# Twelve column tiles of the input projection by Strassen's seven products, in three waves

## The chip, the cores and the metric

The kernel runs on one core of a Trainium2 chip. The metric is the device time of one execution in microseconds (us). A profile is one execution recorded by the hardware profiler; its span runs from the first to the last recorded instruction and is a little shorter than the device time of that execution. Engines: PE is TensorE's matmuls, PEld its weight loads, DVE is VectorE, ACT is ScalarE, POOL is GpSimd, SP is SyncE, from whose queue this kernel starts its transfers.

## The reference

A decoder trunk of two layers over 1024 tokens of width 1024, all float32. Each layer does, cut to what matters:

```
xn   = rms_norm(h, norm_mix)
proj = xn @ w_in                       # 1024 x 1024 by 1024 x 3120
gq, gk, gv, glr, ggate | cc, cb, ch, cgate | cq, ckv, kr, mgate = split(proj)
o_gla  = gated linear attention(gq, gk, gv, glr), normed, times silu(ggate)
o_conv = cb * causal_conv3(cc * ch) * silu(cgate)
o_mla  = softmax attention(rms_norm(cq) @ w_uq, rms_norm(ckv) @ w_ukv, kr) * silu(mgate)
h = h + concat(o_gla, o_conv, o_mla) @ w_out
h = h + cross_attention(rms_norm(h), mem)
```

The last line of the network is one more rms_norm. The change concerns the columns cc, cb, ch, cgate, cq and ckv of `proj`, 256 columns each.

## The kernel before, in words

Activations are kept transposed: a tile is 128 features by 512 tokens, so a layer's activations are 8 feature tiles in 2 halves of the tokens. Each float32 operand is split into a high part in a shorter format and the rest, and one product is three matmuls, high by high, high by low and low by high (`mm3`, L298 to L303). The input projection's columns are laid out as 25 tiles of 128. `win` (L393) computes one of them: it loads the 1024 x 128 weights (512 KB, `wraw`), casts the high part on ScalarE and subtracts it for the low part in two halves on GpSimd or VectorE (`wsplit`; tiles with number 3 modulo 4 go to VectorE), and for each half of the tokens accumulates 8 x 3 matmuls of 128x512 in one PSUM bank, which VectorE evicts with the norm's factor R (L402). Raw weights have 2 buffers (tag "wr"), split parts 6 (tag "w").

Per layer: first the tiles of the linear attention's q, k and v; then its front; then the state loop, `gla_body` for two head pairs in four rounds. In each round the program takes steps from a list called `fill` between the bodies' steps: the attention gates, the linear attention's gates (`gate`, which writes the finished gate to DRAM) and the first convolution group (`conv`, four tiles). After the loop come `latent` for ckv (tiles 20 and 21) and cq (18 and 19), the rotary keys, the first keys and the second convolution group, and then the softmax attention, the output projection and the cross-attention.

Tiles come from pools with tags: "s" has 64 tiles of 128x512, "p" 9, "pt" 4. A new tile waits until one of its tag is free. The eight PSUM banks are tagged "mm" (1), "S" (4), "t" (2) and "v" (1). The order of the instructions on each engine is set before the run by a planner that simulates the program with modelled costs; at run time each engine, and the SP queue, goes through its list in that order and waits where an operand or a buffer is not ready. `hd` in DRAM holds the residual stream, which `absorb` writes for each feature tile.

## Time and profile before

| | us |
|---|---|
| median of 3 runs | 1417.07 |
| lowest, highest | 1415.62, 1418.71 |
| the profiled execution's own time | 1415.69 |
| its span | 1413.9 |
| PE busy in it | 1382.9 |

The span is what the profile's views divide; the profiled execution's own time is 1.8 us longer. PE's busy time counts overlapping matmuls once. A row of grouped instructions ends with the group's busy time, the mean length of one in ns, and the idle time of its engine just before them with what ended it.

### The profile page before, as it was taken

What the parts mean: (1) busy time and instruction counts of PE and PEld (TensorE: products, weight loads), DVE (VectorE), ACT (ScalarE), POOL (GpSimd) and SP (SyncE); (2) the same over time, 40 slices, a digit from 0 to 9 for tenths busy, and PEclk for the clock granted to TensorE, in tenths of its full rate; (3) what the DMA queues carried; (4) which work ended last, traced back from release to release, by engine and by line L of the source; (5) the groups of instructions that cost most, each with busy time, mean ns of one, the idle gap of its engine ahead of it and who ended that gap; (6) DMA issues with size and microseconds to landing.
All of it is one profiled execution on the core that took longest, in us unless ns stands there. A gap on an engine that the chain in (4) does not pass through costs nothing.

```text
span 1413.9 us, 19744 instructions
## 1 busy us (share of the span) xinstructions
PE 1382.9 (98%) x7132; PEld 1128.0 (80%) x7132; DVE 771.0 (55%) x1431; ACT 690.0 (49%) x1462; POOL 571.7 (40%) x584
## 2 busy tenths in 40 slices
PE   7998999999999999999999999999999999999998
PEld 6787888888776688888878788888887767888886
DVE  7846445364788554545653632534657883553533
ACT  5446544253777442555431653424557773344543
POOL 6325335215556452353342532441356663414320
PEclk9999999999999999999999999999999999999999
DMA  8131222122122254321522121211232123534403
GB/s 310 53 129 53 77 76 74 47 63 91 45 61 65 92 172 134 121 89 46 185 100 82 49 78 53 89 58 45 83 86 60 33 81 112 194 105 142 156 1 120
DMA packets 61827, 131.13 MB, mean 93 GB/s; under 512 B 7553, under 2 KB 14497, under 8 KB 61729
## 3 DMA queue, kind: packets, MB, share of 16 engines
q1 hardware_dynamic: 61728, 129.87, 28.5%
q8 instruction: 56, 0.92, 0.3%
q14 instruction: 43, 0.34, 0.1%
HBM read 95.76 MB, written 33.55 MB: 91 GB/s over the span
## 4 chain that ended last, share of the span: by engine, by line
PE 83%; DVE 9%; ACT 3%; issue 2%; DMA 2%; POOL 1%; SPq 0%; DVEq 0%; POOLq 0%; ACTq 0%
PE op_ps L301 4%; PE op_ps L302 4%; PE op_ps L303 4%; PE av L848 4%; PE pt L834 3%; PE xqps L301 2%; PE xqps L302 2%; PE xqps L303 2%; PE s L301 2%; PE gg_ps L301 2%; PE gg_ps L303 2%; PE gg_ps L302 2%; PE s L303 1%; PE s L302 1%; DVE gla_a L479 1%
## 5 line engine op out<-in xcount | busy, mean ns | idle before, releaser
L149 POOL TENSOR_TENSOR win_l<-win_r,win_h 128x512 fp32r<-128x512 f32 x76 | 104.1, 1391 | 196.4 <-ACT win_h L127 191.6
L805 POOL TENSOR_SCALAR p<-p,sm 128x128 f32<-128x128 f32 (+3 forms) x144 | 87.8, 619 | 63.8 <-DVE sm L803 41.5
L127 ACT CAST win_h<-win_r 128x1024 fp32r<-128x1024 f32 x50 | 52.4, 1049 | 123.5 <-PE gg_ps L302 36.6
L303 PE MATMUL op_ps<-mix_h,wout_l 128*128 128x512 f32 x256 | 99.9, 390 | 0.0
L302 PE MATMUL op_ps<-mix_l,wout_h 128*128 128x512 f32 x256 | 99.8, 390 | 0.0
L301 PE MATMUL op_ps<-mix_h,wout_h 128*128 128x512 f32 x256 | 99.0, 393 | 0.0
L799 ACT ACTIVATE p<-s,nm 128x128 f32<-128x128 f32 (+3 forms) x144 | 83.2, 581 | 27.1 <-DVE nm L795 13.8
L791 DVE TENSOR_REDUCE nm<-s 128x1 f32<-128x128 f32 (+3 forms) x144 | 78.4, 551 | 3.1 <-PE s L303 1.1
L834 PE MATMUL pt<-ident,p 128*128 128x128 f32 x432 | 70.6, 280 | 1.6 <-POOL p L805 1.5
L834 PEld LDWEIGHTS pt<-ident,p 128*128 128x128 f32 x432 | 49.7, 140 | 27.3 <-issue 13.7
L848 PE MATMUL av<-ph,V 128*64 128x256 f32 x480 | 69.6, 375 | 0.0
L149 POOL TENSOR_TENSOR wout_l<-wout_r,wout_h 128x512 fp32r<-128x512 f32 x32 | 43.3, 1376 | 42.5 <-ACT wout_h L127 34.4
L301 PE MATMUL s<-k_h,q_h 128*128 128x128 f32 (+3 forms) x144 | 55.2, 386 | 1.3 <-ACT p L799 0.6
L301 PEld LDWEIGHTS op_ps<-mix_h,wout_h 128*128 128x128 f32 x256 | 47.7, 188 | 10.5 <-issue 0.8
L302 PEld LDWEIGHTS op_ps<-mix_l,wout_h 128*128 128x128 f32 x256 | 48.1, 188 | 9.9
L303 PEld LDWEIGHTS op_ps<-mix_h,wout_l 128*128 128x128 f32 x256 | 48.1, 188 | 9.8
L842 ACT COPY ph<-pt 128x512 f32<-128x512 f32 (+1 forms) x72 | 39.6, 549 | 23.7 <-PE pt L834 20.6
L301 PE MATMUL xqps<-op_x_h,wq_h 128*128 128x512 f32 x128 | 51.1, 399 | 0.0
L1005 POOL TENSOR_SCALAR xp<-xp,xsm 128x256 f32<-128x256 f32 x64 | 29.8, 482 | 51.4 <-DVE xsm L1003 51.3
L303 PE MATMUL xqps<-op_x_h,wq_l 128*128 128x512 f32 x128 | 50.4, 393 | 0.0
L302 PE MATMUL xqps<-op_x_l,wq_h 128*128 128x512 f32 x128 | 50.2, 392 | 0.0
L302 PE MATMUL s<-k_l,q_h 128*128 128x128 f32 (+3 forms) x144 | 49.9, 347 | 0.0
(502 smaller groups left out, 4292.5 us busy)
## 6 DMA issues: line engine op xcount, KB each, us to landing
win_r<-in_w_in SPq DMA_DIRECT2D x50, 512.0 KB, 3.6
wout_r<-in_w_out SPq DMA_DIRECT2D x16, 512.0 KB, 4.0
x<-in_x SPq DMA_DIRECT2D x16, 256.0 KB, 6.3
hd<-h SPq DMA_DIRECT2D x16, 256.0 KB, 4.0
op0r<-hd SPq DMA_DIRECT2D x16, 256.0 KB, 4.0
hd<-op0r SPq DMA_DIRECT2D x16, 256.0 KB, 2.9
wq_r<-in_w_mem SPq DMA_DIRECT2D x8, 512.0 KB, 3.8
wk_r<-in_w_mem SPq DMA_DIRECT2D x8, 512.0 KB, 3.6
```

The costliest lines, as they stand in the source:

```text
L127: ins = self.nc.scalar.copy(hi, raw)
L149: eng.tensor_tensor(lo, src, hi.bitcast(F32), op=ALU.subtract)
L301: nc.tensor.matmul(ps, a[0], b[0], start=first, stop=False, **k)
L302: nc.tensor.matmul(ps, a[0], b[1], start=False, stop=False, **k)
L303: nc.tensor.matmul(ps, a[1], b[0], start=False, stop=last, **k)
L791: nc.vector.tensor_reduce(nm[:, b : b + 1], ps[:, :w], axis=AX.X, op=ALU.max, negate=True)
L799: nc.scalar.activation(x[:, :w], ps[:, :w], AF.Exp, bias=nm[:, 0:1], accum_out=sm[:, b : b + 1])
L805: nc.gpsimd.tensor_scalar(pr[b][:, :w], pr[b][:, :w], sm[:, 0:1], 1.0, op0=ALU.mult, op1=ALU.mult)
L834: nc.tensor.transpose(ps[:, o : o + P], prob[qi][kt // 4][:, (kt % 4) * P : (kt % 4 + 1) * P], self.ident,)
L842: nc.scalar.copy(pt[:, :w], ps[:, :w])
L848: nc.tensor.matmul(av[own if j == 0 else other, q0:256], self.V[kt][:, 64 * h : 64 * h + 64], pt[:, j * 256 : j * 256 + 256 - q0], start=( ...
L1005: nc.gpsimd.tensor_scalar(pr[:, j], pr[:, j], sm[:, j : j + 1], 1.0, op0=ALU.mult, op1=ALU.mult)
```

## The change

Twelve tiles per layer leave `win`: the latents' four (18 to 21) and the two convolution groups' eight (10 to 17), as six pairs. For a pair, the output is a 2 x 2 block (two column tiles, two token halves) and the sum over features is cut in two halves of four tiles. Instead of eight block products, each 4 x 3 matmuls, there are seven, by Strassen's scheme in Winograd's form: four sums of activation blocks (`a_side`) and four differences of weight blocks (`w_first`, `w_second`) go into them, and partial products are added to each other as they leave PSUM.

The seven products are done in three waves over all six pairs. `wave1` does three of them with the plain activations and writes two partial products per pair to DRAM (`pd`), the second weights' differences too (`wtd`). `wave2` does two with the sums S2 and S3, reads the partial products back and writes two new ones (`ud`). `wave3` does two with S1 and S4 and reads those. Results go to `Sink` tiles, the convolution's gates through DRAM. `a_side` reads the residual stream from `hd`, scales it by gain and by R, and writes the four sums to DRAM (`sd`); `s_parts` reads and splits them. `conv` and `latent` no longer compute their tiles but take the sinks. The linear attention's gates move ahead of the convolution in `fill`; `a_side`, `wave1` and two of `s_parts` are put into the state loop's rounds. Buffers: "s" from 64 to 59, "pt" from 4 to 5, raw weights from 2 to 4.

```diff
-BUFS = {"s": 64, "p": 9, "pt": 4, "tq": 1}
+BUFS = {"s": 59, "p": 9, "pt": 5, "tq": 1}
...
+PAIRS = ((20, 21), (18, 19), (10, 11), (13, 12), (14, 15), (17, 16))
...
-        raw = self.wp.tile(shape, F32, tag="wr", bufs=2, name=name + "_r")
+        raw = self.wp.tile(shape, F32, tag="wr", bufs=4, name=name + "_r")
...
+    def a_side(self, l):
+        nc = self.nc
+        for k in range(4):
+            t = {}
+            for m, c in ((k, 1), (k + 4, 1), (k, 0), (k + 4, 0)):
+                x = self.g(f"sa{l}_{m}_{c}")
+                nc.sync.dma_start(x, self.hd[m][c])
+                nc.scalar.activation(x, x, AF.Copy, scale=self.gain(l, "mix", m))
+                self.mul(nc.gpsimd, x, x, self.R[c])
+                t[(m // 4, c)] = x
+            a11, a12, a21, a22 = t[(0, 0)], t[(1, 0)], t[(0, 1)], t[(1, 1)]
+            nc.vector.tensor_tensor(a22, a21, a22, op=ALU.add)
+            nc.gpsimd.tensor_tensor(a21, a11, a21, op=ALU.subtract)
+            nc.vector.tensor_tensor(a11, a22, a11, op=ALU.subtract)
+            nc.gpsimd.tensor_tensor(a12, a12, a11, op=ALU.subtract)
+            for j, x in enumerate((a22, a11, a21, a12)):
+                nc.sync.dma_start(self.sd[j][k], x)
+            yield
+    def s_parts(self, l, j):
...
+        for k in range(4):
+            raw = self.g(f"sr{l}_{j}_{k}", tag="pt")
+            nc.sync.dma_start(raw, self.sd[j][k])
+            hi, lo = self.g(f"sh{l}_{j}_{k}", F32R), self.g(f"sl{l}_{j}_{k}", F32R)
+            self.split(hi, lo, raw, eng=self.pick("sp", k))
...
+    def w_first(self, l, n):
...
+        r1, r2 = raws
+        hi, lo = self.wsplit(r1, sh, f"win{l}_{i1}")
+        nc.gpsimd.tensor_tensor(r2[:, :4], r2[:, :4], r1[:, :4], op=ALU.subtract)
+        nc.gpsimd.tensor_tensor(r2[:, 4:], r2[:, 4:], r2[:, :4], op=ALU.subtract)
+        t4 = self.g(f"t4_{l}_{n}", tag="tq", shape=[P, 4, P])
+        nc.vector.tensor_tensor(t4, r1[:, 4:], r2[:, 4:], op=ALU.subtract)
+        nc.sync.dma_start(self.wtd[n], r2)
+        w4 = self.wp.tile(sh, F32R, tag="w", bufs=6, name=f"w4_{l}_{n}")
+        nc.scalar.copy(w4[:, :4], t4)
+        self.sub(nc.vector, w4[:, 4:], t4, w4[:, :4])
...
+    def w_second(self, l, n, j):
...
+        if j == 0:
+            nc.sync.dma_start(r, src)
+            (nc.vector if n % 2 else nc.gpsimd).tensor_tensor(r[:, 4:], r[:, 4:], r[:, :4], op=ALU.subtract)
+            nc.sync.dma_start(r[:, :4], self.wtd[n][:, 4:])
+        else:
+            nc.sync.dma_start(r[:, :4], self.wtd[n][:, :4])
+            nc.sync.dma_start(r[:, 4:], src[:, 4:])
...
+        nc.scalar.copy(hi, r)
+        for h, e in ((0, nc.gpsimd), (4, nc.vector)):
+            self.sub(e, lo[:, h : h + 4], r[:, h : h + 4], hi[:, h : h + 4])
...
+    def wave1(self, l):
...
+        w = self.w_first(l, 0)
+        for n in range(len(PAIRS)):
...
+            self.prod(x, wb, a11, True)
+            p1 = self.g(f"p1_{l}_{n}", tag="pt")
+            nc.vector.tensor_tensor(p1, x, self.R[0], op=ALU.mult)
+            nc.sync.dma_start(self.pd[n][0], p1)
+            yield
+            if n + 1 < len(PAIRS):
+                w = self.w_first(l, n + 1)
+            self.prod(y, w4, a22, True)
...
+            nc.sync.dma_start(self.pd[n][1], p4)
+            yield
+            self.prod(x, lambda k: wb(4 + k), a12, False)
+            s = self.sink[PAIRS[n][0]]
+            nc.vector.tensor_tensor(s.tile(0), x, self.R[0], op=ALU.mult)
+            s.done(0)
+            yield
...
+    def wave2(self, l):
...
+        def head(n):
+            w[n] = self.w_second(l, n, 0)
+            x[n] = self.psum(("S", "mm", "S", "t")[n % 4], f"vx{l}_{n}")
+            p1[n] = self.spilled(l, f"q1_{l}_{n}", self.pd[n][0])
+            self.prod(x[n], w[n][0], s2, True)
+            u = self.g(f"u2_{l}_{n}", tag="pt")
+            nc.vector.tensor_tensor(u, x[n], p1[n], op=ALU.add)
+            nc.sync.dma_start(self.ud[n][0], u)
+        head(0)
+        yield
+        for n in range(N):
+            if n + 1 < N:
+                head(n + 1)
+                yield
+            p4 = self.spilled(l, f"q4_{l}_{n}", self.pd[n][1])
+            self.prod(x[n], w[n][1], s3, False)
+            u = self.g(f"u3_{l}_{n}", tag="pt")
+            nc.vector.tensor_tensor(u, x[n], p1[n], op=ALU.add)
+            nc.sync.dma_start(self.ud[n][1], u)
+            k = self.sink[PAIRS[n][0]]
+            nc.gpsimd.tensor_tensor(k.tile(1), u, p4, op=ALU.add)
+            k.done(1)
+            yield
+    def wave3(self, l):
...
+        def head(n):
+            w[n] = self.w_second(l, n, 1)
...
+            u3 = self.spilled(l, f"v3_{l}_{n}", self.ud[n][1])
+            self.prod(y[n], w[n][0], s1, True)
...
+            nc.vector.tensor_tensor(k.tile(1), y[n], u3, op=ALU.add)
...
             gates = [self.gate(l, 22 + i, self.mgd[i], f"mg{l}_{i}") for i in range(3)]
+            gates += [self.gate(l, 7 + i, self.ggd[i], f"gg{l}_{i}") for i in range(3)]
...
+            sides = self.a_side(l)
+            first = self.wave1(l)
+            fill = chain(*gates[1:])
+            parts = chain(self.s_parts(l, 1), self.s_parts(l, 2))
             bodies = [self.gla_body(l, 0), self.gla_body(l, 1)]
-            for _ in range(4):
+            for r in range(4):
                 for b in bodies:
                     next(b, None)
+                    next(sides, None)
+                    if r > 1:
+                        next(parts, None)
+                        next(parts, None)
                     for _ in range(2):
-                        next(fill, None)
+                        if next(fill, 0) == 0:
+                            next(first, None)
+                            next(first, None)
             for b in bodies:
                 run(b)
-            run(fill)
+            run(sides)
+            weave((first, 1), (parts, 1))
+            last_parts = chain(self.s_parts(l, 0), self.s_parts(l, 3))
+            weave((self.wave2(l), 1), (last_parts, 1))
...
+            third = self.wave3(l)
+            for _ in range(10):
+                next(third, None)
             self.wkn = self.mla_w(l, 2)
-            for _ in range(2):
-                next(conv)
             run(self.krope(l))
+            run(third)
             run(self.mla_k(l, 0))
```

## Rows read from the trace of the kernel before

**Rows 1.** The page: span, and busy time of each engine with its share.
```profile
span 1413.9 us, 19744 instructions
PE 1382.9 (98%) x7132; PEld 1128.0 (80%) x7132; DVE 771.0 (55%) x1431; ACT 690.0 (49%) x1462; POOL 571.7 (40%) x584
```

**Rows 2.** The page: the chain that ended last, share of the span by engine.
```profile
PE 83%; DVE 9%; ACT 3%; issue 2%; DMA 2%; POOL 1%; SPq 0%; DVEq 0%; POOLq 0%; ACTq 0%
```

**Rows 3.** Windows: state loop, then to first keys; layer 1's loop.
```profile
core 0: us, PE busy (x) PEld busy (x) DVE busy (x) ACT busy (x) POOL busy (x), PEclk, DMA share, GB/s
137.00:251.50 114.50, 114.25 (x606) 98.12 (x605) 47.17 (x86) 50.34 (x104) 45.79 (x38) 1.00 0.22 70
251.50:345.00 93.50, 93.03 (x410) 76.63 (x409) 46.17 (x63) 37.17 (x57) 25.90 (x20) 1.00 0.21 65
823.00:937.50 114.50, 114.25 (x607) 98.07 (x606) 47.10 (x86) 50.46 (x103) 45.78 (x38) 1.00 0.22 70
```

**Rows 4.** Timeline of PE in the latents: start us, length us, instruction.
```profile
252.21 0.39 PE L301 MATMUL ckv_ps<-h_x_h,win_h 128*128 128x512 f32 x1
...
257.65 0.39 PE L301 MATMUL ckv_ps<-h_x_h,win_h 128*128 128x512 f32 x1
```

**Rows 5.** Groups of GpSimd, 137 to 251.5 us: busy us, mean ns, idle before.
```profile
L149 POOL TENSOR_TENSOR win_l<-win_r,win_h 128x512 fp32r<-128x512 f32 x14 | 18.4, 1335 | 27.5 <-ACT win_h L127 27.5
L152 POOL TENSOR_TENSOR osq<-osb 128x384 f32<-128x384 f32 x8 | 6.6, 826 | 10.7 <-ACT osb L579 10.7
L152 POOL TENSOR_TENSOR gg<-gg,gg_1s 128x512 f32<-128x512 f32 x2 | 2.6, 1284 | 14.2 <-issue 14.2
```

**Rows 6.** Groups of VectorE in the same stretch.
```profile
L590 DVE TENSOR_TENSOR gv<-osb,oms 128x192 f32<-128x192 f32 x14 | 6.8, 525 | 2.6 <-ACT oms L586 2.6
L402 DVE TENSOR_TENSOR gg<-gg_ps,h_acc 128x512 f32<-128x512 f32 x6 | 4.1, 690 | 15.0 <-PE gg_ps L303 15.0
L412 DVE SCALAR_TENSOR_TENSOR gg_2s<-gg,gg_2s 128x512 f32<-128x512 f32 x2 | 1.9, 950 | 0.9 <-ACT gg_2s L411 0.9
L412 DVE SCALAR_TENSOR_TENSOR gg_1s<-gg,gg_1s 128x512 f32<-128x512 f32 x2 | 1.4, 693 | 0.9 <-ACT gg_1s L411 0.9
L149 DVE TENSOR_TENSOR win_l<-win_r,win_h 128x512 fp32r<-128x512 f32 x2 | 1.3, 684 | 0.0
```

**Rows 7.** Groups of ScalarE over the whole span.
```profile
L127 ACT CAST win_h<-win_r 128x1024 fp32r<-128x1024 f32 x50 | 52.4, 1049 | 123.5 <-PE gg_ps L302 36.6 <-PE gq_ps L302 24.9 <-PE gk_ps L302 16.1
L159 ACT CAST q_h<-tq 128x512 fp32r<-128x512 f32 x24 | 14.9, 620 | 18.1 <-DVE tq L769 17.8
L162 ACT ACTIVATE op_x_h<-op1r,gains 128x512 fp32r<-128x512 f32 x16 | 11.5, 720 | 21.8 <-DVE op1r L926 21.8
```

**Rows 8.** Waits, 130 to 345 us: total us, times, longest.
```profile
POOL win_l L149 <- ACT win_h L127: 58.1, 8, 15.4
```

**Rows 9.** Transfers, 130 to 345 us: total; one issue line.
```profile
DMA packets 7459, 14.70 MB, mean 68 GB/s; under 512 B 893, under 2 KB 2941, under 8 KB 7446
win_r<-in_w_in SPq DMA_DIRECT2D x12, 512.0 KB, 3.6
```

**Rows 10.** The page's transfers: a 256 KB load from the residual stream.
```profile
op0r<-hd SPq DMA_DIRECT2D x16, 256.0 KB, 4.0
```

**Rows 11.** Windows in which the DMA engines are full.
```profile
11.00:16.00 5.00, 4.61 (x15) 3.06 (x14) 4.84 (x6) 4.76 (x8) 4.92 (x4) 1.00 1.04 403
512.00:518.00 6.00, 6.00 (x28) 4.99 (x27) 5.75 (x6) 3.01 (x6) 5.40 (x4) 1.00 1.00 361
690.00:700.00 10.00, 9.64 (x43) 7.66 (x42) 8.84 (x11) 8.03 (x13) 8.00 (x6) 1.00 1.00 347
```

**Rows 12.** Waits of the SP queue, 130 to 345 us.
```profile
SPq L595 <- DVE gv L590: 43.6, 10, 10.2
SPq L120 <- ACT win_h L127: 40.6, 7, 14.9
```

**Rows 13.** GpSimd's weight subtraction: ns min/median/max.
```profile
L149 POOL TENSOR_TENSOR win_l<-win_r,win_h x76: 1264/1299/1927, 11.0 to 1015.0; 128x512 fp32r<-128x512 f32 x76
```

More of the change, by code (lines that the diff above doesn't have):

```diff
@@ new lines, in s_parts, with prod @@
+    def s_parts(self, l, j):
+        nc = self.nc
+        self.Sp[j] = []
+        for k in range(4):
[3 more added lines that the diff above has]
+            self.split(hi, lo, raw, eng=self.pick("sp", k))
+            self.Sp[j].append((hi, lo))
+            yield
+    def prod(self, ps, w, xs, first):
+        for k, x in enumerate(xs):
+            self.mm3(ps, w(k), x, first and k == 0, k == len(xs) - 1, skip_group_check=True)
@@ new lines, in wave1 @@
+    def wave1(self, l):
+        nc = self.nc
+        half = lambda j, c: [(self.x1[4 * j + k][0][c], self.x1[4 * j + k][1][c]) for k in range(4)]
+        a11, a12, a22 = half(0, 0), half(1, 0), half(1, 1)
+        w = self.w_first(l, 0)
+        for n in range(len(PAIRS)):
+            tags = ("S", "S") if n % 2 else ("mm", "S")
+            x = self.psum(tags[0], f"wx{l}_{n}")
+            y = self.psum(tags[1], f"wy{l}_{n}")
+            wb, w4 = w
+            self.prod(x, wb, a11, True)
[6 more added lines that the diff above has]
+            self.prod(y, w4, a22, True)
+            p4 = self.g(f"p4_{l}_{n}", tag="pt")
+            nc.vector.tensor_tensor(p4, y, self.R[1], op=ALU.mult)
+            nc.sync.dma_start(self.pd[n][1], p4)
[5 more added lines that the diff above has]
+            yield
@@ new lines, in wave3 @@
+    def wave3(self, l):
+        nc = self.nc
+        s1, s4 = self.Sp[0], self.Sp[3]
+        N = len(PAIRS)
+        w, y = {}, {}
+        def head(n):
+            w[n] = self.w_second(l, n, 1)
+            y[n] = self.psum(("S", "mm", "S", "t")[n % 4], f"vy{l}_{n}")
+            u3 = self.spilled(l, f"v3_{l}_{n}", self.ud[n][1])
+            self.prod(y[n], w[n][0], s1, True)
+            k = self.sink[PAIRS[n][1]]
+            nc.vector.tensor_tensor(k.tile(1), y[n], u3, op=ALU.add)
+        head(0)
+        yield
+        for n in range(N):
+            if n + 1 < N:
+                head(n + 1)
+                yield
+            u2 = self.spilled(l, f"v2_{l}_{n}", self.ud[n][0])
+            self.prod(y[n], w[n][1], s4, False)
+            k = self.sink[PAIRS[n][1]]
+            nc.vector.tensor_tensor(k.tile(0), y[n], u2, op=ALU.add)
+            k.done(0)
+            k.done(1)
+            yield
+            if n in self.after:
+                yield from self.after[n]
@@ L431, in in_q, with sinks @@
+    def sinks(self, l):
+        self.sink = {}
+        for j in range(2):
+            self.sink[13 + 4 * j] = GateSink(self, self.cgd[j], f"cg{l}_{j}")
+            for i in range(3):
+                self.sink[10 + 4 * j + i] = Sink(self, f"c{i}{l}_{j}")
+        for i in range(18, 22):
+            self.sink[i] = Sink(self, f"lat{l}_{i}")
     def in_q(self, l, p, tags=("mm", "S")):
@@ L672, in latent @@
         nc = self.nc
-        raw = [self.g2(f"{what}{l}_{i}") for i in range(2)]
+        raw = [self.sink[base + i].t for i in range(2)]
         acc = self.g2(f"{what}acc{l}", tag="pt")
         for i in range(2):
-            c = 0
-            for _ in self.win(l, base + i, f"{what}{l}_{i}", lambda c: raw[i][c], PAIR[f"lat{i}"]):
+            for c in range(2):
                 if i == 0:
```

103 lines of the change are left out of this document (66 added, 37 removed).

## The prediction

> **What bounds the kernel now.** I read the page's share of busy time first, then the chain of waits, then the busy times of the two stretches that the change rewrites, then the single instructions and transfers in them. The page has TensorE busy in 98% of the 1413.9 us span [rows 1], and the chain that ended last runs on PE for 83% of it [rows 2]. In the stretches that hold the state loop with its fill (137 to 251.5 us) and the latents, the second convolution group and the first keys (251.5 to 345 us), PE is busy for 114.25 of 114.5 us and 93.03 of 93.5 us at full clock; VectorE, ScalarE and GpSimd are at most half busy and the DMA engines are at 0.21 to 0.22. Layer 1's loop shows the same numbers [rows 3]. So in these stretches time is the number of matmuls times their spacing. A 128x512 matmul is shown as 0.39 us, but its records overlap: 24 of them in a row take from 252.21 to 257.65 us, start to start, which is 5.44/24 = 0.2267 us each [rows 4]. That is the price of one.
>
> **The change part by part.** *TensorE.* A column tile is 2 halves x 8 k x 3 matmuls = 48; twelve tiles are 576 per layer. A pair by seven products is 7 x 4 x 3 = 84, six pairs 504. So 72 matmuls go per layer, 72 x 0.2267 = 16.3 us, and 32.6 us in both. The waves then take 216, 144 and 144 matmuls: 49.0, 32.6 and 32.6 us of PE. The product order gives each accumulation a product (2.7 us) in which its eviction hides.
>
> *GpSimd.* Added per layer: 24 operations of 128x512 for the sums of the activations, 24 in the first weights, 15 in the second and third, 8 in splitting the sums, 6 in the second wave: 77. Gone: the subtractions of nine of the twelve tiles, 18 (three were VectorE's). Net 59 x 1.335 us [rows 5] = 79 us. All the cover there is: GpSimd was busy 45.8 + 25.9 us in the two stretches [rows 3], 208 us long; after it is 151 of 192. What counts is the first part, loop and first wave. It lasts 114.5 - 4 x 48 x 0.2267 + 49.0 = 120 us of PE. GpSimd has there 52 new operations (69.4 us at 1.335), the gates' six subtractions, twelve gate products at about 1.285 and eight squares at 0.826 [rows 5]: 99.5 us, 83%. It sits idle for 58.1 us in eight waits before a weight's subtraction today [rows 8]; that cushion is nearly used up.
>
> *VectorE and ScalarE.* VectorE: 18 more evictions at 0.69, 12 + 15 for weights, 8 + 8 for the sums, less 6: 55 x 0.69 [rows 6] = 38 us per layer on top of 93 in 208. ScalarE: weight casts from 12 x 1.05 to about 22 us, 16 scalings at 0.72 and 16 casts at 0.62 [rows 7]: 31 us more on top of 88. Neither becomes a bound; both hide behind PE as long as their inputs arrive. What is queued behind a late one is the state loop's own eviction and copy.
>
> *DMA.* This is the larger change. The old stretch moves 14.70 MB at a mean of 68 GB/s [rows 9]. Added per layer: 16 loads and 16 stores of 256 KB for the sums, 16 loads to split them, six 512 KB stores and twelve 256 KB stores in the first wave, and in the second wave per pair 512 + 256 + 256 + 256 KB of loads and 2 x 256 KB of stores. The second wave thus moves 6 x 1.835 MB, 8 x 0.262 MB of sums for the third wave and 0.52 MB of gates: 13.6 MB in 32.6 us, which is 418 GB/s. With all 16 engines busy the trace shows 361 and 347 GB/s where loads and stores mix, 403 GB/s where nearly all are loads [rows 11]. 13.6 MB takes 39.2 us at 347 and 33.8 us at 403. So the second wave is short by 1.2 to 6.6 us per layer, less what is fetched ahead: two of the four raw weight buffers (1 MB, 2.9 us at 347) are free when the first wave ends, and the last stores may land in the third wave, which moves some 7.5 MB in 32.6 us (230 GB/s). From below the cost is 0, from above 6.6; I take 3 per layer, nearest to the mixed rows less one prefetch.
>
> *Queue and pool.* All transfers go through SP in order. SP waits today 43.6 us for the state's results and 40.6 us for weight casts without harm [rows 12], because a weight is due only every 10.9 us. Now some 130 more issues stand in the same queue, stores that wait for a result among loads that are due; each wait holds every load behind it. And the pool "s" has 59 tiles: the activations hold 32, the state loop's q, k and v 20, its transposed keys 2 and the rotary rows 2, so 3 are free where the sums want 4 at a time. The first sum therefore waits for the first round of the state loop to give tiles back, and the rest crowds into rounds 3 and 4, where the first weights want GpSimd too. Bounds: 0 if the plan slides under PE, 20 us per layer if GpSimd's 99.5 us become serial with a fifth idle. I take 3. The fewer tiles in the output projection (32 + 32 wanted at its end) cost nothing: the old tiles come free at two per 0.68 us, just as they are wanted. For the third wave and the hand-overs between waves I take 1.5 (nothing at best; at worst one weight load, 3.6 us [rows 9], at each of two hand-overs).
>
> *Sum.* Profiled execution 1415.7 - 32.6 + 2 x (3 + 3 + 1.5) = 1398.1 us. That execution lies 1.4 us under the median of the three runs shown, so I say 1398.
>
> **A rule against it.** VectorE and GpSimd slow each other where both read SBUF: a VectorE gate step of one form took 0.950 us on one tile and 0.693 us on another [rows 6], and one GpSimd subtraction form took from 1264 to 1927 ns [rows 13]. The Trainium skill ("SBUF — State Buffer", section "Who interferes with whom") states that a VectorE instruction with two SBUF inputs and a GpSimd one that reads SBUF lock each other out for the whole instruction. The spread in these rows agrees with it; that every overlap blocks fully they do not show.
>
> **The rivals.** *All hidden:* the planner keeps the transfers and sums under PE as it does now with everything else. For: 98% PE at present, and no idle PE at 137 to 345 us. Against: 418 GB/s is more than any row shows for a mix. Time 1415.7 - 32.6 = 1383.1.
>
> *The shared read port binds the first part:* VectorE's instructions with two SBUF inputs there (12 for weights, 8 sums, 4 splits, 12 gate steps, 2 gate-weight subtractions at about 0.69, 16 at 0.525) are 34.6 us; GpSimd at 1.27, near the least of one form [rows 13], is 95 us. In turn they take 130 us against PE's 120: 10 us per layer instead of my 3. With 4.5 for the rest, 1415.7 - 32.6 + 29 = 1412. For: the rows just named. Against: the means are near the minimum today.
>
> *The second wave runs at the pace of its weights (slower):* its second operand is loaded (3.6 us for 512 KB [rows 9]), differenced (1.3), half of it overwritten by a second load that must wait for that difference (4.0 for 256 KB [rows 10]), cast (1.05) and subtracted (1.3): 11.3 us in series, through one in-order queue, against 5.44 us of PE per pair. Buffers allow about three pairs ahead. If the queue lets it be only one (a store that waits for an eviction stands before the next load), each of 12 pairs waits 11.3 - 5.4 = 5.9 us: 1415.7 - 32.6 + 71 = 1454. It decides from a lead under 8.6 us, where 12 x 2.7 us eats the gain; a lead of 7 us gives 1435. For: DMA engines near full lengthen both loads. Against: the four raw buffers.
>
> *The change does less than it says:* the matmuls are counted out in the code, so I give this no chance.
>
> **How the numbers follow.** My forecast (1390 to 1408) 0.50, all hidden 0.17, the shared port (1408 to 1425) 0.15, the second wave's chain (1420 to 1455) 0.18. What a measurement of this kernel can tell from no change is about 0.2%, 2.8 us. Faster: 0.50 + 0.17 + a third of the port case, about 0.72. Within 0.2%: 0.07 out of the port case. Slower: the chain and the port's tail, 0.21. Range 1383 to 1424: it holds the first three cases and the mild end of the fourth; about 0.17 is above it, some 0.03 below.
>
> **What would show it.** 144 fewer 128x512 matmuls at the same spacing. In the second wave, some 32 to 40 us long per layer, a DMA share near 1 and PE gaps that end with a weight's subtraction or cast which itself waited for a transfer: that is my 3 us. In the state loop, GpSimd at 80% or more, with the sums' products late in it. If PE is without gaps, all is hidden; if PE waits in the first part behind GpSimd while the DMA share is moderate, the port rival holds; if SP's waits in the second wave are for evictions and PE waits over 2.7 us per pair, the chain does. I am wrong if PE idles over 16 us per layer in these stretches, or if stages that the change does not touch move by more than a few us.

## The result and the profile after

The changed kernel takes 1466.2 us (median of four runs, 1462.4 to 1468.6) against 1417.0 us in four runs of the kernel before: a ratio of 1.034 with an interval of 1.032 to 1.037, 49 us slower. The page of the changed kernel, first the span, the busy times and the granted clock by slices:

```profile
span 1466.0 us, 20485 instructions
PE 1381.8 (94%) x6988; PEld 1117.5 (76%) x6988; DVE 897.6 (61%) x1541; ACT 741.3 (51%) x1550; POOL 752.6 (51%) x702
PEclk9999999997999999999999999999799999999999
```

The mean granted clock over the span, of the changed kernel and of the kernel before:

```profile
core 0: 1466.0 us, clock 0.973
```

```profile
core 0: 1413.9 us, clock 0.997
```

Against [rows 1] there are 144 matmuls fewer, as the prediction counted, but PE's busy time is the same, 1381.8 for 1382.9 us. An estimate from the two clocks accounts for that: (1382.9 - 32.6) x 0.997/0.973 = 1383.6. So of the 85 us between the forecast gain and the span (52.1 + 32.6), some 53 are PE standing (84.2 us for 31.0) and, by this estimate, some 32 its work at a lower granted clock. The windows of the changed kernel's layer 0, cut at the first instruction of each stage in PE's timeline (state loop with first wave; second wave; third wave up to the first attention scores; the first 29 us of the attention):

```profile
core 0: us, PE busy (x) PEld busy (x) DVE busy (x) ACT busy (x) POOL busy (x), PEclk, DMA share, GB/s
136.10:266.00 129.90, 121.74 (x617) 103.23 (x618) 84.35 (x113) 66.41 (x130) 102.05 (x75) 0.97 0.66 227
266.00:299.00 33.00, 33.00 (x145) 26.87 (x144) 22.18 (x24) 11.56 (x16) 20.06 (x15) 1.00 1.00 339
299.00:370.90 71.90, 57.04 (x215) 44.10 (x213) 47.67 (x64) 36.49 (x58) 36.38 (x27) 0.86 0.51 169
370.90:400.00 29.10, 24.70 (x133) 19.79 (x134) 20.21 (x59) 17.44 (x51) 15.74 (x20) 0.88 0.19 58
```

and of layer 1, whose fourth row is the whole attention up to its gates' first matmul (gmps):

```profile
847.40:979.40 132.00, 122.64 (x617) 103.66 (x618) 85.72 (x113) 66.51 (x130) 102.70 (x75) 0.96 0.66 222
979.40:1012.40 33.00, 32.93 (x146) 26.95 (x145) 21.85 (x25) 11.55 (x16) 20.48 (x15) 1.00 0.99 346
1012.40:1083.20 70.80, 54.95 (x216) 42.34 (x214) 47.68 (x64) 36.38 (x58) 36.30 (x27) 0.88 0.52 172
1083.20:1202.30 119.10, 114.43 (x683) 83.52 (x683) 96.70 (x270) 84.56 (x230) 73.43 (x97) 0.97 0.20 55
```

The reader is to see three things. PE stands 8 us in the loop and 15 us behind the second wave, where before it stood 0.25 and 0.5 us [rows 3]. The second wave, with every DMA engine full, has no gap (0.07 us in layer 1). And where PE has stood, the granted clock is under 1.

What each stage should have taken follows from the kernel before. The loop with its fill was 114.1 us there (from 137.4, the first transposed key, to 251.5); less four conv tiles, plus the first wave, that is the prediction's 120. From 251.5 to the first scores (351.6) it was 100.1; less eight tiles (87.0) and plus the third wave (32.6) that is 45.7. The attention up to gmps took 112.7. So, in us for layer 0 (layer 1 in brackets):

| stage | PE's price | measured | lost |
|---|---|---|---|
| state loop and first wave | 120.0 | 129.9 (132.0) | 9.9 (12.0) |
| second wave | 32.6 | 33.0 (33.0) | 0.4 (0.4) |
| third wave to first scores | 45.7 | 71.9 (70.8) | 26.2 (25.1) |
| attention to gmps | 112.7 | 119.4 (119.2) | 6.7 (6.5) |

The losses add up to 87 us; less the 32.6 gained that is 55, and the span grew by 52.1. No other stage moved by more than a few us. The largest new waits of PE in the changed kernel (total us, times, longest):

```profile
PE cq_ms L296 <- ACT cq_ah L193: 13.6, 4, 6.4
PE o L783 <- DVE gg L436: 13.2, 6, 4.2
PE vy L335 <- DVE c L628: 10.4, 4, 2.9
```

**The loop, read closely.** Groups of VectorE and GpSimd in the changed kernel's loop (136 to 266 us):

```profile
L815 DVE TENSOR_TENSOR gv<-osb,oms 128x192 f32<-128x192 f32 x16 | 14.9, 973 | 5.2 <-ACT oms L811 5.2
L487 DVE TENSOR_TENSOR sa<-sa,sa 128x512 f32<-128x512 f32 x4 | 6.7, 1685 | 5.4 <-POOL sa L486 5.4
...
L183 POOL TENSOR_TENSOR win_l<-win_r,win_h 128x512 fp32r<-128x512 f32 x16 | 24.1, 1529 | 3.5 <-ACT gg_1s L447 3.5
L186 POOL TENSOR_TENSOR sa<-sa,h_acc 128x512 f32<-128x512 f32 x16 | 22.4, 1416 | 9.5 <-ACT sa L481 9.5
```

The step gv, which took 525 ns [rows 6], takes 973; GpSimd's subtraction 1529 for 1335 [rows 5]. VectorE stands for GpSimd's sums and GpSimd for ScalarE's scalings. Most of PE's 8 us of standing in this loop is one wait, which comes three times; none of its waits there ends with a transfer, and the last is at 217 us:

```profile
PE o L783 <- DVE gg L436: 6.6, 3, 3.8
```

The longest of the three in the timeline of the changed kernel (start, length, instruction, idle time before it). ScalarE, which takes the scalings as their loads land, with the norm's small steps (oms) among them:

```profile
180.90 0.72 ACT L481 ACTIVATE sa<-sa,gains 128x512 f32<-128x512 f32 x1 [0.86 <-DMA sa<-hd]
181.53 0.28 ACT L810 ACTIVATE oms<-oms,eps 128x4 f32<-128x4 f32 x1
181.72 0.71 ACT L481 ACTIVATE sa<-sa,gains 128x512 f32<-128x512 f32 x1
182.33 0.19 ACT L811 ACTIVATE oms<-oms 128x4 f32<-128x4 f32 x1
```

then VectorE, and PE:

```profile
182.56 1.97 DVE L815 TENSOR_TENSOR gv<-osb,oms 128x192 f32<-128x192 f32 x2 [2.90 <-ACT oms L811]
184.45 0.68 DVE L436 TENSOR_TENSOR gg<-gg_ps,h_acc 128x512 f32<-128x512 f32 x1
```

```profile
181.03 0.39 PE L336 MATMUL gg_ps<-h_x_l,win_h 128*128 128x512 f32 x1
185.18 0.46 PE L783 MATMUL o<-gv,atb 128*128 128x96 f32 x2 [3.76 <-DVE gg L436]
```

The eviction gg takes R and PE's product, whose last recorded matmul ends at 181.4. Yet it stands in VectorE's order behind gv, gv behind a step of ScalarE, and that behind a scaling whose load has just come. (Whether the tile that gg writes was free before, no row shows.)

**The third wave, read closely.** Windows of the changed kernel within the third row above, and PE around its longest wait:

```profile
320.00:330.00 10.00, 3.72 (x15) 2.34 (x13) 7.70 (x11) 9.45 (x17) 3.70 (x3) 0.78 0.24 79
330.00:345.00 15.00, 10.04 (x29) 7.21 (x29) 10.05 (x17) 7.43 (x13) 0.00 (x0) 0.73 0.18 57
```

```profile
328.34 0.80 PE L296 MATMUL cq_ms<-cq_ah,ones 128*128 128x512 f32 x1 [5.53 <-ACT cq_ah L193]
329.89 0.80 PE L296 MATMUL cq_ms<-cq_ah,ones 128*128 128x512 f32 x1 [0.76 <-ACT cq_ah L193]
330.48 0.63 PE L335 MATMUL vy<-sh,w2h 128*128 128x512 f32 x1
...
335.18 0.63 PE L337 MATMUL vy<-sh,w2l 128*128 128x512 f32 x1
```

By 320 us the third wave has given its first two pairs to the latents' norms. The norm's sum cq_ms stands in PE's order ahead of the next products; its input passes through ScalarE, busy 9.45 of 10 us, and VectorE in turns. PE works 3.72 of those 10 us, and the twelve products that follow are 0.427 us apart ((335.18 - 330.48)/11) instead of 0.2267 [rows 4]. The weights of these products were complete at 326.06, with VectorE's last step on a second weight before 345 us:

```profile
324.31 1.75 DVE L183 TENSOR_TENSOR w2l<-w2r,w2h 128x512 fp32r<-128x512 f32 x1
```

So for some 4.4 us, to 330.48, the norm's sum stood ahead of products whose weights were ready; before that the weights were late as well. Then the reverse: VectorE has the latents' steps ahead of the eviction that frees a bank for PE:

```profile
338.50 2.49 DVE L898 TENSOR_TENSOR lat<-lat,cqacc 128x512 f32<-128x512 f32 x4
341.02 0.68 DVE L183 TENSOR_TENSOR krp<-kr,krp 64x512 fp32r<-64x512 f32 x1
341.74 2.74 DVE L197 SCALAR_TENSOR_TENSOR cqp_l<-lat,gains,cqp_h 128x512 fp32r<-128x512 f32 x4
344.39 0.68 DVE L628 TENSOR_TENSOR c<-vy,v 128x512 f32<-128x512 f32 x1
```

### The profile page after: what moved, and what is told of

Same layout as the page of the kernel before. It is cut to its first block, busy times and chain, and to the rows that moved or that the text cites. A ratio compares the mean times of both kernels' runs of the same rounds, so it can differ in the third digit from the quotient of the medians.

```text
span 1466.0 us, 20485 instructions
## 1 busy us (share of the span) xinstructions
PE 1381.8 (94%) x6988; PEld 1117.5 (76%) x6988; DVE 897.6 (61%) x1541; ACT 741.3 (51%) x1550; POOL 752.6 (51%) x702
## 5 line engine op out<-in xcount | busy, mean ns | idle before, releaser
L183 POOL TENSOR_TENSOR win_l<-win_r,win_h 128x512 fp32r<-128x512 f32 x64 | 96.0, 1522 | 81.0 <-ACT win_h L161 70.1
L1011 POOL TENSOR_SCALAR p<-p,sm 128x128 f32<-128x128 f32 (+3 forms) x144 | 87.2, 615 | 69.1 <-DVE sm L1009 33.3
L1040 PE MATMUL pt<-ident,p 128*128 128x128 f32 x432 | 71.9, 282 | 0.3
L161 ACT CAST win_h<-win_r 128x1024 fp32r<-128x1024 f32 x38 | 39.6, 1046 | 62.2 <-PE gq_ps L336 22.8
L335 PE MATMUL vy<-sh,w2h 128*128 128x512 f32 x96 | 42.2, 439 | 10.4 <-DVE c L628 10.4
L337 PE MATMUL s<-k_h,q_l 128*128 128x128 f32 (+3 forms) x144 | 49.4, 352 | 2.6 <-DVE q_l L183 2.6
L326 POOL TENSOR_TENSOR op_acc<-op_acc,op_sq 128x512 f32<-128x512 f32 x16 | 23.5, 1475 | 52.5 <-ACT op_sq L325 52.5
```

Of the source, the lines that this page charges most:

```text
L161: ins = self.nc.scalar.copy(hi, raw)
L183: eng.tensor_tensor(lo, src, hi.bitcast(F32), op=ALU.subtract)
L335: nc.tensor.matmul(ps, a[0], b[0], start=first, stop=False, **k)
L337: nc.tensor.matmul(ps, a[1], b[0], start=False, stop=last, **k)
L1011: nc.gpsimd.tensor_scalar(pr[b][:, :w], pr[b][:, :w], sm[:, 0:1], 1.0, op0=ALU.mult, op1=ALU.mult)
L1040: nc.tensor.transpose(ps[:, o : o + P], prob[qi][kt // 4][:, (kt % 4) * P : (kt % 4 + 1) * P], self.ident,)
```

## The experiments

Thirteen kernels ran, each of them the changed kernel with the edit shown, in two runs that lie up to 6.4 us apart (noside). The kernels noside, nosidelate and latenoconv leave out work that the result needs. The stages of all, layer 0, in us, cut as above:

| kernel | loop, first wave | second wave | third wave to scores | attention | time, median | ratio to before |
|---|---|---|---|---|---|---|
| changed kernel | 129.9 | 33.0 | 71.9 | 119.4 | 1466.2 | 1.032 to 1.037 |
| pt7 | 132.4 | 39.1 | 66.9 | 122.2 | 1487.0 | 1.047 to 1.053 |
| pt7p7 | 128.6 | 38.2 | 65.5 | 121.9 | 1467.2 | 1.032 to 1.040 |
| latplain | 162.8 | 21.3 | 53.0 | 118.7 | 1468.5 | 1.034 to 1.040 |
| mixwave | 130.7 | 21.8 | 98.1 | 118.6 | 1495.0 | 1.052 to 1.060 |
| late | 128.2 | 33.3 | 63.3 | 119.4 | 1450.3 | 1.021 to 1.028 |
| lateconv | 130.0 | 33.5 | 55.6 | 131.6 | 1458.5 | 1.027 to 1.033 |
| latenoconv | 128.8 | 33.5 | 61.1 | 117.7 | 1443.7 | 1.015 to 1.025 |
| nosaload | 134.9 | 32.7 | 70.7 | 119.8 | 1473.1 | 1.037 to 1.043 |
| noside | 119.9 | 34.2 | 71.7 | 119.6 | 1448.2 | 1.017 to 1.029 |
| stt | 127.3 | 33.9 | 68.7 | 119.7 | 1465.7 | 1.032 to 1.038 |
| poolsum | 134.8 | 39.9 | 68.9 | 119.8 | 1489.6 | 1.049 to 1.055 |
| latestt | 128.3 | 33.9 | 63.5 | 120.1 | 1451.2 | 1.022 to 1.028 |
| nosidelate | 122.8 | 33.2 | 63.3 | 120.1 | 1432.7 | 1.009 to 1.015 |

The loop is the same code in the changed kernel and late, lateconv and latenoconv, and takes 128.2 to 130.0 there; in noside and nosidelate, which share theirs, 119.9 and 122.8. A difference of 3 us in that column means nothing. (In latplain the loop's column holds four latents' tiles as well and the waves four pairs; in mixwave the second and third waves are interleaved.)

### First: is it buffers, cover, or the sums' loads? (pt7, late, nosaload, latplain)

**pt7**: two more buffers of the pool that the latents, the convolution and the gates share, paid for with a raw weight buffer.

```diff
-BUFS = {"s": 59, "p": 9, "pt": 5, "tq": 1}
+BUFS = {"s": 59, "p": 9, "pt": 7, "tq": 1}
...
-        raw = self.wp.tile(shape, F32, tag="wr", bufs=4, name=name + "_r")
+        raw = self.wp.tile(shape, F32, tag="wr", bufs=3, name=name + "_r")
...
```

> Seven tiles in the pool "pt" instead of five, paid for by three raw weight buffers instead of four. Theory 1 (the latents' norm chain, with the third wave's evictions queued behind it on VectorE, leaves PE without work): the chain is as long as before, 1466 us within 6. Rival (the pool "pt", shared by the chain, the gates, the spilled sums and the raw sums, holds the steps back): PE's waits in the third wave shrink by 10 us a layer or more, 1446 us or less.

Slower, 1487.0, neither theory's number. The wait at cq_ms fell from 13.6 to 4.9 us, but PE now waits 7.5 us for weights in the second wave, which took 39.1 instead of 33.0. Two edits were mixed here; pt7p7 below keeps the four raw buffers.

**late**: the latents' norms and the convolution's epilogue behind the third wave.

```diff
-            self.after = {
-                1: chain(self.latent(l, "ckv", 20), self.latent(l, "cq", 18)),
-                3: self.conv(l, 0),
-            }
+            self.after = {}
             conv = self.conv(l, 1)
-            third = self.wave3(l)
-            for _ in range(10):
-                next(third, None)
+            run(self.wave3(l))
+            run(self.latent(l, "ckv", 20))
+            run(self.latent(l, "cq", 18))
+            run(self.conv(l, 0))
             self.wkn = self.mla_w(l, 2)
             run(self.krope(l))
-            run(third)
```

> Latents' norms and the first convolution group are taken out of the third wave and put behind it. Theory 1: the third wave runs as tight as the second (about 33 us from its first to its last matmul, no PE wait for its evictions), and the same chain then stands uncovered behind it; in all 1466 us within 15. Rival (transfers or weight buffers slow the third wave itself): the wave stays at 45 us or more from first to last matmul, and the time rises by the chain, 1490 us or more.

16 us faster than the changed kernel, just outside theory 1's 1466 within 15. Windows of late from the third wave to the scores:

```profile
297.10:330.00 32.90, 32.27 (x142) 26.25 (x141) 22.91 (x28) 19.57 (x30) 23.34 (x16) 1.00 0.65 216
330.00:360.40 30.40, 21.05 (x75) 13.86 (x73) 28.46 (x36) 17.44 (x29) 16.57 (x12) 0.91 0.56 172
```

The third wave now runs with 0.6 us of gaps at full clock. What was beside it stands behind it, where VectorE is busy 28.46 of 30.4 us and PE 21.05: there VectorE is the bound, with the norms, the key's and query's low parts and the convolution's products in one row. So the latents' steps need not be early; they only must not stand ahead of ready products. A third of the stage's 26 us goes that way (8.6 us, 7.5 in layer 1); the other two thirds, 17.6 us a layer, stand in the part that VectorE fills. Some of VectorE's time there is longer steps: two of its four products lat take 1.6 us each in late, beside GpSimd's steps, where the four in the changed kernel's row above took 0.6 each while GpSimd did nothing (330 to 345 us).

```profile
335.38 3.15 DVE L898 TENSOR_TENSOR lat<-lat,cqacc 128x512 f32<-128x512 f32 x2 [0.93 <-ACT cqacc L299]
```

**nosaload**: the sums are built from the split activations already in SBUF, without loads and without ScalarE.

```diff
-                nc.sync.dma_start(x, self.hd[m][c])
-                nc.scalar.activation(x, x, AF.Copy, scale=self.gain(l, "mix", m))
-                self.mul(nc.gpsimd, x, x, self.R[c])
+                xh, xl = self.x1[m]
+                nc.gpsimd.tensor_tensor(x, xh[c].bitcast(F32), xl[c].bitcast(F32), op=ALU.add)
+                self.mul(nc.vector, x, x, self.R[c])
```

> The sums of the activations are built from the split parts that lie in SBUF (one add on GpSimd in place of its product, the product with R on VectorE) instead of from loads of the residual stream with a scaling on ScalarE. GpSimd does as much as before. Theory 2 (late loads hold ScalarE and VectorE in the state loop, and the gate's eviction that frees a PSUM bank is queued behind): PE's waits in the state loop fall by 6 to 10 us a layer, 1446 to 1454 us. Rival (GpSimd's load, or its port shared with VectorE, holds the loop): no fall, 1464 to 1475 us.

No gain: the loop took 134.9, and the time, 1473.1, is the rival's. Without these loads and without ScalarE's scalings the loss stays. But the edit also puts 16 products on VectorE, so it does not show that the late loads in the timeline above cost nothing.

**latplain**: the four latents' tiles by plain products behind the first wave, four conv pairs in the waves.

```diff
-PAIRS = ((20, 21), (18, 19), (10, 11), ...
+PAIRS = ((10, 11), ...
...
-            weave((first, 1), (parts, 1))
+            weave((first, 1), (parts, 1), (chain(self.latent(l, "ckv", 20), self.latent(l, "cq", 18)), 1))
...
-            for _ in range(10):
+            for _ in range(2):
                 next(third, None)
```

> The four tiles of the latents go back to plain products behind the first wave, and only the four pairs of the convolution go through the waves; 24 matmuls more per layer, 10.9 us in all. Theory 1: the latents' chain is covered by the second and third wave, the 26 us of waiting per layer around the third wave go to 5 or less: 1466 + 11 - 42 = 1435 us. Rival (transfers, buffers or the waves themselves cause it): 1466 + 11 less a third of the waits, 1460 us or more.

No gain in all: 1468.5, where theory 1 said 1435. The 48 matmuls more cost 10.9 us by PE's price, so the rest of the kernel took 8.6 us less. From third wave to scores the loss against PE's price (45.7 less the two pairs' 10.9) fell from 26 to 18 us a layer; in layer 0 the loop's rose from 10 to 16. With the latents done long before, PE now waits 16.7 us in two waits of up to 9.0 for the rotary key's parts, which stand in VectorE's order, while products of the third wave are queued behind:

```profile
PE yps L912 <- DVE krp L183: 16.7, 2, 9.0
```

The edit itself moved the rotary keys, from behind ten of the third wave's steps to behind two. Cover that is there by count helps less where the order puts a late step ahead of it.

### Second: the sums themselves, and what can stand behind the third wave (noside, lateconv, latenoconv, mixwave)

**noside**: the sums left out.

```diff
-            nc.sync.dma_start(raw, self.sd[j][k])
+            nc.sync.dma_start(raw, self.hd[k + 4 * (j % 2)][j // 2])
...
-            sides = self.a_side(l)
...
                 for b in bodies:
                     next(b, None)
-                    next(sides, None)
...
-            run(sides)
```

> The sums of the activations are left out: their loads, scalings, products, adds and stores; the third-party tiles that are split in their place are tiles of the residual stream, so the matmuls are the same in number and their results are not the projection's. Theory 3 (the sums' steps, put among the state loop's in the queues of ScalarE, VectorE and GpSimd, cost the loop its waits): the second wave starts 6 to 10 us earlier in layer 0 and as much more in layer 1, 1446 to 1454 us. Rival (the first weights and the first wave's own steps do it): under 3 us a layer, 1460 us or more.

18 us faster, as theory 3 said; the second wave starts 11 us earlier in layer 0, for its 6 to 10. The window of noside's loop, and gv in it:

```profile
134.80:254.70 119.90, 117.85 (x616) 100.21 (x617) 63.84 (x105) 56.75 (x114) 67.27 (x51) 1.00 0.52 176
```

```profile
L815 DVE TENSOR_TENSOR gv<-osb,oms 128x192 f32<-128x192 f32 x16 | 8.5, 571 | 2.3 <-ACT oms L811 2.3
```

The loop takes 119.9 us, PE's price to 0.1 us, with the whole first wave, its weights and its stores in it; in layer 1 it takes 122.9 for 132.0. The loop's loss is the sums, all of it in layer 0 and 9 of 12 us in layer 1. VectorE has 8 instructions fewer, worth 12.7 us by the two sa groups (6.7 and 6.0), and is busy 20.5 us less: the others became shorter too, gv from 973 to 571 ns. The sums' loads and stores went with them; no run parts the stores from the arithmetic.

**lateconv**: late (the edit is shown against it), and the convolution's epilogue inside the attention, a step after each unit from the seventh on.

```diff
-            run(self.conv(l, 0))
...
-            run(conv)
+            self.convs = chain(self.conv(l, 0), conv)
...
             yield from self.mla_tail(l, h, ip)
+            if n >= 6:
+                next(self.convs, None)
```

> As the run with the latents' norms and the convolution behind the third wave (1450 us), but the convolution's steps are put into the softmax attention, from its seventh unit on. Theory 4 (what is left to do when the third wave ends is a chain on VectorE, and the convolution's steps stand in it): 6 to 10 us a layer less between the third wave and the attention, of which the attention gives some back, 1432 to 1442 us. Rival (the chain is that of latents, keys and queries alone, the convolution fills its gaps): 1448 to 1456 us.

Slower than late, and neither number. The scores come 7.7 us earlier than in late (55.6 for 63.3), and the attention is 12.2 us longer (8.6 in layer 1), with a new wait of PE:

```profile
PE s L335 <- ACT p L1005: 11.8, 13, 1.6
```

The work moved out of a stage bound by VectorE fell into one that has no room for it.

**latenoconv**: late (the edit is shown against it) without VectorE's shifted products of the convolution.

```diff
-            for s in (1, 2):
+            for s in ():
                 nc.vector.scalar_tensor_tensor(
```

> As the run with the latents' norms and the convolution behind the third wave, but the convolution's shifted products on VectorE are left out (two or three per half and group). Theory 4: PE's waits between third wave and attention fall by 5 to 8 us a layer, 1434 to 1440 us. Rival: 1447 us or more.

6.6 us faster than late, between the two numbers; the stage to the scores gave 2.2 us a layer of it and the attention 1.7. The convolution's products are a part of VectorE's row, not most of it.

**mixwave**: the first two pairs' third wave before the last two pairs' second wave, and the latents' norms beside that.

```diff
-            weave((self.wave2(l), 1), (last_parts, 1))
+            weave((self.wave2(l, (0, 1, 2, 3)), 1), (last_parts, 1))
...
+            run(self.wave3(l, (0, 1)))
+            weave((self.wave2(l, (4, 5)), 1), (chain(self.latent(l, "ckv", 20), self.latent(l, "cq", 18)), 1))
+            third = self.wave3(l, (2, 3, 4, 5))
...
```

> As the changed kernel, but the latents' two pairs go through the third wave before the last two pairs go through the second, so that their norms have 33 us of other products to hide behind instead of 22. Theory 1 (the norm chain lacks cover): waits around the third wave from 26 to 14 us a layer or less, 1438 to 1446 us. Rival (the order in the queues is the fault, whatever the cover): 1460 us or more.

1495.0 us, the slowest of all, on the side of the rival. PE in it, and VectorE's last step on a weight before 346 us:

```profile
337.61 0.80 PE L296 MATMUL cq_ms<-cq_ah,ones 128*128 128x512 f32 x1 [11.73 <-ACT cq_ah L193]
...
343.61 0.63 PE L335 MATMUL vy<-sh,w2h 128*128 128x512 f32 x1
...
316.28 1.16 DVE L183 TENSOR_TENSOR w2l<-w2r,w2h 128x512 fp32r<-128x512 f32 x1
```

PE stands 11.7 us at the norm's sum. The products that follow at 343.61 use weights whose parts were written by 317.4 us (no step on a second weight follows until 346), and sums that earlier pairs had used. By weights and sums they were ready, and they stood behind it in the order. Cover at hand was not what was missing here: in that form the cover theory fell.

### Third: which engine's share of the sums, and buffers again (stt, poolsum, pt7p7, latestt)

**stt**: scaling and product of each of the 16 sum inputs as one VectorE instruction.

```diff
-                nc.scalar.activation(x, x, AF.Copy, scale=self.gain(l, "mix", m))
-                self.mul(nc.gpsimd, x, x, self.R[c])
+                nc.vector.scalar_tensor_tensor(
+                    x, x, self.gain(l, "mix", m), self.R[c], op0=ALU.mult, op1=ALU.mult
+                )
```

> The change with one edit: each of the 16 first steps of the sums in a layer (scale by the norm's gain on ScalarE, then the product with the row norm on GpSimd) becomes one VectorE instruction that does both. GpSimd and ScalarE have 16 instructions fewer in the state loop, VectorE 16 more. Leaving the sums out altogether moved the start of the second wave from 266.0 to 254.7 us, so 11.3 us a layer lie in them. Theory A (GpSimd's load: its products and VectorE's steps lengthen each other, and the chains that alternate between the two are held up): 16 x 1.3 us = 21 us less on GpSimd, the second wave starts at 258 to 262, the time is 1450 to 1458. Theory B (VectorE's queue: the loop's evictions stand in order behind the steps of the sums): 16 x 0.7 = 11 us more in that queue, the second wave starts at 268 to 276, the time is 1470 to 1486.

**poolsum**: VectorE's two operations of each quarter of the sums on GpSimd.

```diff
-            nc.vector.tensor_tensor(a22, a21, a22, op=ALU.add)
+            nc.gpsimd.tensor_tensor(a22, a21, a22, op=ALU.add)
...
-            nc.vector.tensor_tensor(a11, a22, a11, op=ALU.subtract)
+            nc.gpsimd.tensor_tensor(a11, a22, a11, op=ALU.subtract)
```

> The change with the opposite edit: the two additions and subtractions of each quarter of the sums that stood on VectorE go to GpSimd, so that VectorE has 8 instructions fewer a layer in the state loop and GpSimd 8 more (8 x 1.3 = 10 us). Theory A (GpSimd's load and the lengthening): the second wave starts at 268 to 274 instead of 266.0, the time is 1470 to 1482. Theory B (VectorE's queue): it starts at 260 to 264, the time is 1454 to 1462.

The loops of stt and of poolsum:

```profile
135.00:262.30 127.30, 120.49 (x617) 102.53 (x618) 87.26 (x129) 56.55 (x114) 81.69 (x59) 0.97 0.68 230
```

```profile
135.30:270.20 134.90, 122.61 (x617) 103.28 (x617) 67.90 (x103) 66.16 (x130) 106.73 (x83) 0.96 0.61 208
```

stt takes 20 us from GpSimd and 10 from ScalarE and adds 2.9 to VectorE, and the time is the same (1465.7), between both theories' numbers: neither alone. VectorE's other steps did become shorter, gv to 690 ns (135 to 254 us; 1007 in the changed kernel in the same stretch):

```profile
L816 DVE TENSOR_TENSOR gv<-osb,oms 128x192 f32<-128x192 f32 x14 | 9.1, 690 | 1.2 <-ACT oms L812 1.2
```

The wait only moved, from o to the next matmul (up) behind the same eviction gg, 4.1 us at most. poolsum takes 16 us of busy time from VectorE, adds 5 to GpSimd, and is 23 us slower than the changed kernel, above theory A's range and far from B's: PE waits up to 5.2 us for ScalarE's copy osb and the second wave is late too. So of these two moves the one to GpSimd cost time and the one to VectorE did not, but the sums' cost is not one engine's busy time. The timeline of the loop above shows what it is in one wait: a chain across three engines, in queues that the loop uses for its own steps.

**pt7p7**: the buffers of pt7, paid for with two of the attention's and the spilled products'.

```diff
-BUFS = {"s": 59, "p": 9, "pt": 5, "tq": 1}
+BUFS = {"s": 59, "p": 7, "pt": 7, "tq": 1}
```

> The change with seven instead of five buffers of the pool that the latents, the convolution and the third wave's gates share, paid for with two buffers of the pool of the attention's probabilities and spilled products, so that the four raw weight buffers stay (the run with three of them was slower, and two edits were mixed in it). Theory 1 (the third wave stands because its steps wait for one another's buffers of this pool): TensorE's wait at the norm's sum of the query latent falls from 13.6 us to under 6 for both layers, the first scores stand 5 to 9 us earlier than 370.9, the time is 1448 to 1458, unless the attention pays for its two probability buffers (its 119.4 us a layer would then be 2 to 6 longer). Theory 2 (the steps stand because each engine takes them in a fixed order, whatever buffers there are): within 3 us of 370.9 and 1463 to 1470.

The same time, 1467.2, as theory 2 said, but from other terms. Third wave to scores fell by 6.4 us to 65.5, as the buffer theory said; the second wave rose by 5.2 (PE waits 3.0 us for weights' low parts) and the attention by 2.5. Buffers of this pool are a part of the third wave's loss; what pays for them costs as much.

**latestt**: late and stt together (both edits as above).

> The change with two edits: the latents' norms and the convolution's epilogue behind the third wave (which alone gave 1450.3 us), and the first steps of the sums as one VectorE instruction each. Theory A (GpSimd's load in the state loop): the two gains lie in different stages and add, 1434 to 1442. Theory B (VectorE's queue): 1454 to 1470. Either way it stays slower than the kernel before: the hand-over behind the third wave, some 13 us a layer longer than expected, is untouched by both.

1451.2, late's time, between the theories' numbers: stt adds nothing there either.

### Fourth: one loss or two? (nosidelate)

Both edits, noside's and late's, as above.

> Two edits at once on the change: the sums of the activations are left out of the state loop (the second and third waves then split tiles of the residual stream, so the output is not the reference's), and the latents' norms and the convolution's epilogue stand behind the third wave. Alone they gave 1448.2 and 1450.3 us against 1466.2. If the two losses are separate (the sums' work in the state loop; the order and missing cover behind the second wave), the gains add: the second wave starts at 253 to 256, the first scores stand 62 to 65 us after the third wave's start, and the time is 1432.3 by the sum, 1428 to 1437. If both are one loss (VectorE and GpSimd short of time over the whole stretch, so that what is saved in one stage is asked for in the next), the second edit adds little: 1442 to 1450.

1432.7 against 1432.3 by the sum, nearer than the runs' spread can tell. The two losses are separate: the sums in the loop, 18 us in both layers, and the latents' steps among the third wave's products, 16 us. It still stands 16 us above the kernel before: behind the third wave its scores come 17.6 us a layer later than PE's price (63.3 for 45.7) and its attention takes 7 us a layer more, together more than the 32.6 gained.

## Why the prediction was wrong

The sign was wrong: 1398 forecast, range 1383 to 1424, 1466.2 measured.

- *Matmuls, 32.6 us:* right. 144 went, and the second wave's 144 take 33.0 us.
- *Second wave, 3 us:* 0.4 measured. The DMA engines were full, as forecast, at a share of 1.00:

```profile
DMA packets 5955, 11.20 MB, mean 339 GB/s; under 512 B 662, under 2 KB 812, under 8 KB 5952
```

  11.2 of the 13.6 MB move within it, the rest before and after. That the four raw buffers hold the lead is argued, not shown: with three of them pt7 took 39.1 us, but pt7p7 with four took 38.2. The rival of the weights' chain, whose time came nearest (1454), is refuted in its place: PE has no wait there. It was near by accident.
- *State loop, sums, queue and pool, 3 us:* mis-sized; 9.9 and 12.0 measured. noside puts all of it on the sums. The prediction saw the price in the rival of the shared read port (10 us per layer in the first part), and part of its mechanism shows: with the sums, gv takes 973 ns, without them 571, and 525 before. The Trainium skill ("SBUF — State Buffer", section "Who interferes with whom") states that a VectorE instruction with two SBUF inputs contends with a GpSimd instruction that reads SBUF; the direction agrees with these rows. But stt, with 20 us less on GpSimd and gv at 690 ns, gained nothing, so the longer steps alone are not the bound; the order on the queues, which the wait above shows, is the other part. How the 10 us divide between the two is open. The pool of tiles was not what the prediction took it for: the sums did not wait for the loop's first round, the first four scalings start at 139.3 us and the last ends at 186.4, in the first half of a loop that runs to 266.
- *Third wave and hand-overs, 1.5 us:* **the step that failed**, 26 us a layer, and 6.7 in the attention's start that had no term. It was priced as weight loads at the joints of waves. What was not asked is which work loses its cover when twelve tiles end in one wave. Before, the query latent's norm sum came at 301.5 us and PE went on with the second convolution group until 344.4, under which norms, low parts and evictions went unseen; now each output is finished only by its pair's product in the third wave, and all that depends on them comes at once. The sentence "Neither becomes a bound; both hide behind PE as long as their inputs arrive" summed VectorE over 208 us. In late's 30 us behind the third wave it is busy 94%. In the changed kernel the same steps are set among the products in each engine's fixed order and hold PE up instead; late shows that this part alone was 16 us for both layers. What the lost cover costs by itself, the 17.6 us a layer that stay in late, is read from VectorE's share there; no run takes it away.
- *The attention, 0:* 6.7 a layer. The kernel before in the first 28 us of its attention:

```profile
351.60:380.00 28.40, 28.37 (x170) 22.84 (x169) 20.94 (x66) 21.20 (x61) 15.81 (x24) 1.00 0.23 59
```

  170 matmuls at full clock there, 133 in 29.1 us at 0.88 in the changed kernel. With late's better third wave it is still 119.4 us: it starts behind a PE that has stood, with scores that wait for VectorE's tq and q_l.
- *All hidden:* refuted, though noside shows it true of the first wave by itself.

The prediction named its own test: wrong if PE idles over 16 us a layer. It idles 8 in the loop and 15 behind the second wave, and the attention, which the change does not touch, moved by 6.7. Its sum has no term for the granted clock either, some 32 us by the estimate above. No variant beat the kernel before; the sums' 18 us and the hand-over's loss are together more than the 32.6 that 144 matmuls are worth.

## What to carry to other kernels

A scheme that saves matmuls by finishing many outputs together takes the cover from all that follows them: list, for the stage behind it, the busy time of each other engine against the matmuls that are left there, not against the whole stretch. Extra elementwise work in a stage that PE fills costs its chain's place in the in-order queues before any engine is full: the loop here lost 10 us with GpSimd at 79% and VectorE at 65%. And a step that waits (a norm's sum) should stand behind ready products in PE's order, or it holds them however many there are.

## What the runs showed of the hardware

- All DMA engines full for 33 us at 339 to 346 GB/s, loads and stores mixed, with SBUF in use by every engine, did not delay PE: it was busy for 33.00 and 32.93 of the 33.0 us.
- In a stretch in which PE worked 3.72 of 10 us the granted clock was 0.78, in the next 15 us 0.73, and there twelve matmuls ran 0.427 us apart for 0.2267. These twelve alone so cost 2.4 us more (12 x 0.20) behind a wait of 5.5; over the whole kernel the lower clock is some 32 of the 85 us lost, by the estimate above.
- One VectorE form of 128x192 with two SBUF inputs took 525 ns on average in the kernel before, 973 in the changed kernel's loop, where GpSimd was busy 102 of 130 us, and 571 without the sums, where it was busy 67 of 120. One 128x512 sum took 1685 ns on average in that loop, where a subtraction of the same size took 684 in the kernel before [rows 6].
